# A hybrid decoder step on one core: single PSUM banks for two operands of a seven-product layer, and one table set for logarithm and exponential

## The chip, the cores and the metric

The kernel runs on one core of a Trainium2 chip. The core has five engines that work beside each other: TensorE (PE, the matmuls; PEld is its loading of weights), VectorE (DVE), ScalarE (ACT), GpSimd (POOL) and SyncE (SP, here an issuer of DMAs). Each engine takes its instructions in the order in which they stand in its own queue; semaphores make one engine wait for another. The metric is device microseconds (us) of one execution, as the median of several runs.

## The reference, cut to what matters

One inference step of a two-layer trunk, for a prompt of 512 tokens and 8 samples of one token, which share all weights. Here the two feed-forward halves of a trunk layer matter:

```
def rms_norm(x, g):
    y = x * lax.rsqrt(jnp.mean(x * x, axis=-1, keepdims=True) + EPS)
    return y * g

def swiglu(x, w_in, w_out):                  # w_in 1024 x 5632, w_out 2816 x 1024
    g, u = jnp.split(x @ w_in, 2, axis=-1)
    return (jax.nn.silu(g) * u) @ w_out

def trunk(x, ...):
    for l in range(2):
        x = x + 0.5 * swiglu(rms_norm(x, ffn1_g[l]), ffn1_w_in[l], ffn1_w_out[l])
        x = x + mixer_l(rms_norm(x, mix_g[l]))
        x = x + cross_attn(rms_norm(x, xattn_g[l]), ...)
        x = x + 0.5 * swiglu(rms_norm(x, ffn2_g[l]), ffn2_w_in[l], ffn2_w_out[l])
    return rms_norm(x, final_g)
```

The rest (a convolution and a gated recurrence as the mixer of the first layer, differential attention over paged caches as that of the second, cross-attention) is computed too, and the change does not touch its code, apart from the norm and the PSUM pool that all stages share.

## The kernel before, in words

**Tiles.** The 520 columns (512 prompt tokens, 8 samples) of x lie transposed in eight tiles of 128 x 520. Values are kept in two parts, a rounded high one and a low rest (`ah` and `al` of an activation, `whi` and `wlo` of a weight), so a product takes three passes: `ah,whi`, `al,whi` and `ah,wlo`. Each matmul handles 260 columns; a 520-column result takes a pair of PSUM banks. All eight banks are four such pairs, a pool (`psp`) from which every user takes a whole pair as one tile (`ps()`). What one instruction writes waits for those that still read *the tile*, whichever bank of it they read.

**Feed-forward layers.** Three of the four (`f1_0` and `f2_0` in trunk layer 0, `f1_1` in trunk layer 1) run through `ffn7` (L521). Each has 22 blocks of 128 hidden columns, in chunks of 8, 8 and 6 blocks. A chunk makes the hidden blocks first and then eight *output units*, one for each tile of x (`mm3` of 48 matmuls, `scaled` at L388, an addition to x). A hidden block is made in one of two ways:

- a *plain* one is a g unit and a u unit of 48 matmuls each (L353), then `scaled` of g (L388), Silu (L550), the product of both (L563) and its split into high and low parts (L373, L374). Plain are blocks 0, 1, 2, 8 and 16 of `f1_0` and `f2_0`, and 0, 8 and 16 of `f1_1`;
- a *seven-product layer* (`Seven.run`, 53 of them) makes g and u at once by Strassen's scheme in Winograd's form: seven products of 12 matmuls with sums of the weights (`sums`, `shi`, `slo`) and of the activations (`th`, `tl`) as operands, into four quarter results A, B, C and E. The first pair of banks is the tile `pa` (A and B, a bank each), the second `pc` (C and E).

In short, the order of the products, their destinations and what takes the results out:

```
self.product(A, w["a11"], b(0, 0), True)       # S.copy(g[:, lower], A)            L491
self.product(B, w["s1"], t(0), True)           # S.copy(u[:, upper], B)            L495
self.product(C, w["a12"], b(1, 0), True)       # V.tensor_add(g lower, .., C)      L498
self.product(A, w["s2"], t(1), False)          # S.copy(g[:, upper], A)            L501
self.product(B, w["s4"], b(1, 1), False)       # V.tensor_add, V.tensor_mul        L504, L505
self.product(E, w["a22"], t(3), True)          # S.activation Silu                 L508
self.product(A, w["s3"], t(2), False)          # S.copy, V.tensor_add, V.tensor_add L511 to L513
```

The matmuls of all products are at L472. Afterwards `rest()` multiplies g and u (L517) and splits the product. `Seven.prep` (L425) makes the operands of the next layer, in steps that `run` calls between the products: sums on DVE (L438, L441, L449, L453), casts to the high part on ACT (L439, L442, L446, L450, L455, L457, L461), low parts on DVE (L444, L452, L459, L462). `Seven.operands` (L405) makes the sums of the activations, in steps among the plain units of a first chunk.

**Norm.** `Norm.square` squares x on ACT (L320) and adds on DVE (L321); `_finish` sums over the partitions by two matmuls with a matrix of ones (L339), and makes the inverse root as exp(-0.5 ln(.)) on ACT (L341, L342), when `rstd()` is first asked for. ACT holds one table set of functions; where the next function is not in it, a table load (ACT_TABLE_LOAD) is put ahead.

**What sets the order.** A scheduler places the instructions of each engine by readiness and the order of the code. The products of the layers keep their order by `tc.issue_after`. `Weights` loads and splits weight tiles (L67, L78, L79) some steps ahead of their use, and a list of background work (parameters, at the start) is stepped by `bg.tick`.

Of the kernel before, what the change touches and what calls it, by code (L numbers as in the profile page):

```python
# [8 lines left out]
F32 = mybir.dt.float32  # L9
# [3 lines left out]
AF = mybir.ActivationFunctionType  # L13
# [3 lines left out]
P = 128  # L17
D = 1024
KT = 8
T = 512  # L20
# [30 lines left out]
def halves(ap, n):  # L51
    return ap.rearrange("p (s n) -> p s n", s=2, n=n)
# [122 lines left out]
def build(tc, a, outs):  # L175
# [11 lines left out]
    wspl = ctx.enter_context(tc.tile_pool(name="wspl", bufs=WB))  # L187
    psp = ctx.enter_context(tc.tile_pool(name="psp", bufs=4, space=bass.MemoryType.PSUM))
    drp = ctx.enter_context(tc.tile_pool(name="drp", bufs=1, space=bass.MemoryType.DRAM))
    tmp = ctx.enter_context(tc.tile_pool(name="tmp", bufs=TB))  # L190

    def ps():
        return psp.tile([P, 2, 512], F32, name="ps", tag="ps")

    def t2(name="t2"):
        return tmp.tile([P, TT], F32, name=name, tag="t2")
# [91 lines left out]
    class Norm:  # L288
# [25 lines left out]
        def square(self, k, c0=0, c1=TT):  # L314
            x = xT[k][:, c0:c1]
            if k == 0:
                S.activation(self.ss[:, c0:c1], x, AF.Square)
            else:
                sq = t2("sq")
                S.activation(sq[:, c0:c1], x, AF.Square)  # L320
                V.tensor_add(self.ss[:, c0:c1], self.ss[:, c0:c1], sq[:, c0:c1])  # L321
# [13 lines left out]
        def _finish(self, c0, c1):  # L335
            n = (c1 - c0) // 2
            p = ps()
            for s in range(2):
                PE.matmul(p[:, s, :n], ones, self.ss[:, c0 + s * n:c0 + (s + 1) * n], start=True, stop=True)  # L339
            sd = t2("sd")  # L340
            S.activation(halves(sd[:, c0:c1], n), p[:, :, :n], AF.Ln, bias=eps_t, scale=1.0 / D)  # L341
            S.activation(self._rstd[:, c0:c1], sd[:, c0:c1], AF.Exp, scale=-0.5)  # L342
# [42 lines left out]
    def scaled(p, rstd, name, out=None):  # L385
        n = rstd.shape[-1] // 2
        t = t2(name) if out is None else out
        V.tensor_mul(halves(t[:, :2 * n], n), p[:, :, :n], halves(rstd, n))  # L388
        return t

    class Seven:
# [85 lines left out]
        def run(self, nrm, w, step, before):  # L477
# [6 lines left out]

            pa, pc = ps(), ps()
            A, B, C, E = (p[:, s, :H2] for p in (pa, pc) for s in range(2))
            g, u = t2("g"), t2("u")
# [33 lines left out]
    def ffn7(tag, nrm, post, seven, chunks=CHUNKS, first=iter(())):  # L521

        plain = PLAIN[tag]
        for ci, (f0, nf) in enumerate(chunks):
# [14 lines left out]
            for f in range(f0, f0 + nf):  # L539
# [5 lines left out]
                if f in plain:  # L545
                    pg = ps()
                    for _ in mm3_gen(pg, ws.next((tag, "g", f)), nrm.act, H2):
                        step()
                    g = scaled(pg, nrm.rstd(), "g")
                    S.activation(g, g, AF.Silu)  # L550
                    wu = ws.next((tag, "u", f))
# [4 lines left out]
                    pu = ps()  # L556
                    for _ in mm3_gen(pu, wu, nrm.act, H2):
                        step()
# [106 lines left out]
    with ExitStack() as ctx1:  # L665
# [65 lines left out]
        nmix = Norm("mix", 0)  # L731
        seven = Seven(ctx1.enter_context(tc.tile_pool(name="seven", bufs=1)))
        ffn7("f1_0", n0, nmix.tile_, seven, first=(x for j in range(KT // 2) for x in seven.operands(n0, j)))
        bg.drain()

    def even_mixer(nrm, post):
# [674 lines left out]
    with tc.tile_pool(name="seven", bufs=1) as pool:  # L1411
        seven = Seven(pool)
        n1 = Norm("ffn1", 1, seven=seven)
        ffn7("f2_0", nf, n1.tile_, seven, first=(x for j in range(KT // 2) for x in seven.operands(nf, j)))
        nmix = Norm("mix", 1)
        ffn7("f1_1", n1, nmix.tile_, seven)

    def self_attn_sample(qs, ks, vs, pool, dst, ready, pages, page_order):
# [450 lines left out]
    with tc.tile_pool(name="fin", bufs=2) as pool:  # L1869
# [35 lines left out]
        V.tensor_scalar(ys, ys, r5[:NS, 4:5], None, op0=OP.mult)  # L1905
        S.dma_start(o_ys[:, 0, :], ys.rearrange("p s n -> p (s n)"))
    ctx.close()

# [33 lines left out]
```

## Time and profile before

| | us |
|---|---|
| median of 3 runs | 2598.58 |
| lowest and highest | 2596.54, 2598.66 |
| the profiled execution | 2599.44 |
| span of its trace | 2597.6 |

The profile is one execution, not the median. Its busy times are shares of the span: PE 93%, PEld 88%, DVE 66%, ACT 42%, POOL 10%. These are averages over stages that differ: among the seven-product layers DVE is far busier than in the output units. In the rows further down a matmul of 260 columns lasts 0.28 us, and the next one starts about 0.12 us after it did, so that matmuls overlap; the pace is read from starts. In brackets stands the idle time of an engine ahead of an instruction, and what ended it. The granted clock of PE is given as a share of its upper level: 1.00 is 2.4 GHz and 0.50 is 1.2 GHz.

### The profile page before, as it was taken

What the parts mean: (1) busy time and instruction counts of PE and PEld (TensorE: products, weight loads), DVE (VectorE), ACT (ScalarE), POOL (GpSimd) and SP (SyncE); (2) the same over time, 40 slices, a digit from 0 to 9 for tenths busy, and PEclk for the clock granted to TensorE, in tenths of its full rate; (3) what the DMA queues carried; (4) which work ended last, traced back from release to release, by engine and by line L of the source; (5) the groups of instructions that cost most, each with busy time, mean ns of one, the idle gap of its engine ahead of it and who ended that gap; (6) DMA issues with size and microseconds to landing.
All of it is one profiled execution on the core that took longest, in us unless ns stands there. A gap on an engine that the chain in (4) does not pass through costs nothing.

```text
span 2597.6 us, 49066 instructions
## 1 busy us (share of the span) xinstructions
PE 2425.3 (93%) x20642; PEld 2292.9 (88%) x20642; DVE 1706.8 (66%) x2800; ACT 1097.1 (42%) x1906; POOL 269.1 (10%) x340
## 2 busy tenths in 40 slices
PE   7998999999889998999898999999989899998998
PEld 7898989989868898989898989977889799997898
DVE  7767568995375858478858486699577663354334
ACT  6435244365435525246525244465543232321323
POOL 1000000001021000000000000122011423412410
PEclk9999999999999999999999999999999899998999
DMA  4232333264375323232323233577354766978972
GB/s 141 82 105 83 93 94 112 84 195 146 107 260 165 106 82 100 75 92 84 106 76 95 82 96 116 163 231 234 112 178 143 254 202 217 318 237 277 281 201 66
DMA packets 475150, 382.65 MB, mean 147 GB/s; under 512 B 13590, under 2 KB 435610, under 8 KB 474920
## 3 DMA queue, kind: packets, MB, share of 16 engines
q1 hardware_dynamic: 431456, 224.43, 30.2%
q0 software_dynamic: 43024, 153.93, 17.9%
q8 instruction: 162, 2.65, 0.4%
q10 hardware_dynamic: 448, 1.15, 0.1%
q14 instruction: 60, 0.49, 0.1%
HBM read 363.41 MB, written 16.55 MB: 146 GB/s over the span
## 4 chain that ended last, share of the span: by engine, by line
PE 49%; issue 11%; DVE 7%; DMA 6%; ACT 4%; POOL 1%; ACTq 0%; POOLq 0%; DVEq 0%; another core or an unknown queue 0%
PE ps L353 29%; PE ps L472 14%; DMA page<-in_cache_k_dram,idx 2%; DMA bq<-qxd 1%; DVE pr L1467 1%; PE ps L1525 1%; PE ps L1068 1%; DVE wlo L79 1%; PE ps L652 1%; POOL page L1136 1%; DVE sc L1458 1%; PE ps L1222 1%; ACT g L491 1%; DVE prx L1156 0%; PE ps L1255 0%
## 5 line engine op out<-in xcount | busy, mean ns | idle before, releaser
L353 PE MATMUL ps<-ah,whi 128*128 128x260 f32 (+1 forms) x3936 | 812.7, 288 | 25.0 <-ACT ah L311 9.3
L353 PE MATMUL ps<-al,whi 128*128 128x260 f32 (+1 forms) x3936 | 799.1, 284 | 7.3 <-DVE al L1775 2.6
L353 PE MATMUL ps<-ah,wlo 128*128 128x260 f32 (+1 forms) x3936 | 795.9, 284 | 3.3 <-DVE wlo L79 2.6
L353 PEld LDWEIGHTS ps<-ah,whi 128*128 128x128 f32 x3936 | 609.1, 190 | 49.0 <-issue 16.6
L353 PEld LDWEIGHTS ps<-al,whi 128*128 128x128 f32 x3936 | 610.8, 190 | 13.1 <-DVE al L312 3.1
L353 PEld LDWEIGHTS ps<-ah,wlo 128*128 128x128 f32 x3936 | 609.5, 190 | 7.0 <-DVE wlo L79 4.4
L78 ACT CAST whi<-wraw 128x1024 fp32r<-128x1024 f32 (+1 forms) x254 | 259.2, 1022 | 625.7 <-PE ps L353 443.0
L79 DVE TENSOR_TENSOR wlo<-wraw,whi 128x1024 fp32r<-128x1024 f32 (+1 forms) x254 | 301.4, 1188 | 94.7 <-ACT whi L78 93.1
L472 PE MATMUL ps<-th,shi 128*128 128x260 f32 x636 | 185.4, 292 | 29.4 <-ACT g L491 28.5
L472 PE MATMUL ps<-tl,shi 128*128 128x260 f32 x636 | 179.9, 283 | 0.0
L472 PE MATMUL ps<-th,slo 128*128 128x260 f32 x636 | 179.2, 282 | 0.0
L472 PEld LDWEIGHTS ps<-th,shi 128*128 128x128 f32 x636 | 119.3, 188 | 40.5 <-ACT g L491 39.2
L388 DVE TENSOR_TENSOR t<-ps,rstd 128x520 f32<-128x520 f32 x72 | 50.3, 698 | 131.3 <-PE ps L353 131.3
L652 PE MATMUL ps<-memT,wraw 128*128 128x256 f32 x512 | 122.5, 381 | 0.0
L472 PE MATMUL ps<-al,whi 128*128 128x260 f32 x424 | 120.0, 283 | 0.0
L472 PEld LDWEIGHTS ps<-th,slo 128*128 128x128 f32 x636 | 119.9, 189 | 0.0
L472 PE MATMUL ps<-ah,wlo 128*128 128x260 f32 x424 | 119.9, 283 | 0.0
L472 PEld LDWEIGHTS ps<-tl,shi 128*128 128x128 f32 x636 | 119.8, 188 | 0.0
L472 PE MATMUL ps<-ah,whi 128*128 128x260 f32 x424 | 119.8, 282 | 0.0
L652 PEld LDWEIGHTS ps<-memT,wraw 128*128 128x128 f32 x512 | 92.2, 190 | 10.2
L472 PE MATMUL ps<-ah,shi 128*128 128x260 f32 x212 | 65.7, 310 | 37.7 <-ACT g L501 37.7
L1427 POOL DMA_INDIRECT page<-in_cache_k_dram,idx x64 | 66.3, 1036 | 305.7 <-DVE pr L1467 179.8
(474 smaller groups left out, 4027.5 us busy)
## 6 DMA issues: line engine op xcount, KB each, us to landing
wraw<-in_ffn_w_in_dram SPq DMA_DIRECT2D x176, 512.0 KB
wraw<-in_ffn_w_out_dram SPq DMA_DIRECT2D x64, 512.0 KB
wraw<-in_xattn_w_kv_dram SPq DMA_DIRECT2D x32, 512.0 KB
page<-in_cache_mem_k_dram POOLq DMA_DIRECT2D x32, 512.0 KB
page<-in_cache_mem_v_dram POOLq DMA_DIRECT2D x32, 512.0 KB
page<-in_ffn_w_in_dram POOLq DMA_DIRECT2D x28, 512.0 KB
wraw<-in_ffn_w_out_dram SPq DMA_DIRECT2D x32, 384.0 KB
wraw<-in_attn_w_in_dram SPq DMA_DIRECT2D x24, 512.0 KB
```

Source lines behind the costliest of these rows:

```text
L78: self.nc.scalar.copy(hi[:, :nk], raw[:, :nk])
L79: self.nc.vector.tensor_sub(lo[:, :nk], raw[:, :nk], f32(hi[:, :nk]))
L353: PE.matmul(p[:, s, :n], w[:, j, :], x[:, s * n:(s + 1) * n], start=first and m == 0, stop=last and m == 2)
L388: V.tensor_mul(halves(t[:, :2 * n], n), p[:, :, :n], halves(rstd, n))
L472: e = PE.matmul(dst[:, :H2], wt[:, j, :], x, start=first and j == 0 and m == 0, stop=j == 3 and m == 2, skip_group_check=True)
L491: S.copy(g[:, lower], A)
L652: PE.matmul(p[:, 0, :256], w[:, k, :], memT[:, k, :], start=k == 0, stop=k == KT - 1)
L1068: PE.matmul(p[32 * j:32 * j + 32, o // 4, (o % 4) * P:(o % 4 + 1) * P], inp[:, k, :], w[:, k, :], start=(o % 4 == 0 and k < 4), stop=(k + ...
L1136: G.dma_start(tl, a[src][l, b, t * P:(t + 1) * P].rearrange("p h d -> p (h d)"))
L1222: PE.matmul(dst, self.q[dt][qi][:, qb * P:(qb + 1) * P], self.kp[:, ki, dt, :], start=n == 0, stop=n == 5, skip_group_check=True)
L1427: G.indirect_dma_start(out=t, out_offset=None, in_=src, in_offset=bass.IndirectOffsetOnAxis(ap=idx[:, b * 8 + j:b * 8 + j + 1], axis=0))
L1458: V.reduce_sum(sc[:, j, :].rearrange("p (m h b) -> p h m b", m=2, h=8)[:, :, :, b % 4], pr.rearrange("p (h m d) -> p h m d", h=8, m=2), ax ...
```

## The change

Four things are changed.

1. A function `banks(single)` closes the PSUM pool and opens it anew. With `single` there are two pairs (`psp`) and four single banks (`ps1`), otherwise four pairs as before. `banks(True)` stands ahead of `f1_0` and ahead of `f2_0`; `banks(False)` behind `f1_0` and behind `f1_1`.
2. In `Seven.run` A and B are single banks, a tile each; C and E remain a pair.
3. In `_finish`, where there are single banks, each of the two matmuls with ones has its own bank and its own logarithm of 260 columns. Behind the last square of a norm a preload names the table set `natural_log_exp_and_others`, which holds both functions.
4. In a plain block the scaling of g and its Silu are written into the loop over the u unit: behind the fifth of its eight steps in the first block of a chunk, behind the first step in the others. With the scaling goes `rstd()`, so in the first chunk `_finish` too.

```diff
@@ build
-    psp = ctx.enter_context(tc.tile_pool(name="psp", bufs=4, space=bass.MemoryType.PSUM))
+    psum = {"ctx": ExitStack()}
+
+    def banks(single):
+
+        psum["ctx"].close()
+        psum["ctx"] = ExitStack()
+        psum["two"] = psum["ctx"].enter_context(
+            tc.tile_pool(name="psp", bufs=2 if single else 4, space=bass.MemoryType.PSUM))
+        psum["one"] = None
+        if single:
+            psum["one"] = psum["ctx"].enter_context(tc.tile_pool(name="ps1", bufs=4, space=bass.MemoryType.PSUM))
+
+    banks(False)
...
     def ps():
-        return psp.tile([P, 2, 512], F32, name="ps", tag="ps")
+        return psum["two"].tile([P, 2, 512], F32, name="ps", tag="ps")
+
+    def ps1():
+        return psum["one"].tile([P, 512], F32, name="p1", tag="p1")
@@ Norm.square
-                S.activation(sq[:, c0:c1], x, AF.Square)
+                e = S.activation(sq[:, c0:c1], x, AF.Square)
+                if k == KT - 1 and self.hilo and c1 > T - 1 and c0 == 0:
+                    with tc.issue_after(e.ins):
+                        S.preload_act_table_set("natural_log_exp_and_others")
@@ Norm._finish
-            p = ps()
+            sd = t2("sd")
+            both = None if psum["one"] else ps()
             for s in range(2):
-                PE.matmul(p[:, s, :n], ones, self.ss[:, c0 + s * n:c0 + (s + 1) * n], start=True, stop=True)
-            sd = t2("sd")
-            S.activation(halves(sd[:, c0:c1], n), p[:, :, :n], AF.Ln, bias=eps_t, scale=1.0 / D)
+                c = slice(c0 + s * n, c0 + (s + 1) * n)
+                p = ps1() if both is None else both[:, s]
+                PE.matmul(p[:, :n], ones, self.ss[:, c], start=True, stop=True)
+                if both is None:
+                    S.activation(sd[:, c], p[:, :n], AF.Ln, bias=eps_t, scale=1.0 / D)
+            if both is not None:
+                S.activation(halves(sd[:, c0:c1], n), both[:, :, :n], AF.Ln, bias=eps_t, scale=1.0 / D)
@@ Seven.run
-            pa, pc = ps(), ps()
-            A, B, C, E = (p[:, s, :H2] for p in (pa, pc) for s in range(2))
+            A, B = ps1()[:, :H2], ps1()[:, :H2]
+            pc = ps()
+            C, E = (pc[:, s, :H2] for s in range(2))
@@ ffn7, a plain block
-                    g = scaled(pg, nrm.rstd(), "g")
-                    S.activation(g, g, AF.Silu)
                     wu = ws.next((tag, "u", f))
...
-                    for _ in mm3_gen(pu, wu, nrm.act, H2):
+                    for j, _ in enumerate(mm3_gen(pu, wu, nrm.act, H2)):
+                        if j == (4 if f == f0 else 0):
+                            g = scaled(pg, nrm.rstd(), "g")
+                            S.activation(g, g, AF.Silu)
                         step()
@@ the stages
+        banks(True)
         ffn7("f1_0", n0, nmix.tile_, seven, first=(x for j in range(KT // 2) for x in seven.operands(n0, j)))
         bg.drain()
+        banks(False)
...
+        banks(True)
         n1 = Norm("ffn1", 1, seven=seven)
         ffn7("f2_0", nf, n1.tile_, seven, first=(x for j in range(KT // 2) for x in seven.operands(nf, j)))
         nmix = Norm("mix", 1)
         ffn7("f1_1", n1, nmix.tile_, seven)
+        banks(False)
```

How the instructions stand now is shown at three places. The first is PE in the second seven-product layer of the first chunk of `f1_0`, where the first product ends and the second begins. Before, with `ps_843` the pair of A and B:

```order
L472 MATMUL ps_843<-ah_231,whi_731 128x260
L472 MATMUL ps_843<-al_232,whi_731 128x260
L472 MATMUL ps_843<-ah_231,wlo_732 128x260
L472 MATMUL ps_843<-th_313,shi_771 128x260
L472 MATMUL ps_843<-tl_314,shi_771 128x260
L472 MATMUL ps_843<-th_313,slo_772 128x260
```

Now, with `p1_854` the bank of A and `p1_855` that of B (the line of the matmuls is L495 there):

```order
L495 MATMUL p1_854<-ah_231,whi_742 128x260
L495 MATMUL p1_854<-al_232,whi_742 128x260
L495 MATMUL p1_854<-ah_231,wlo_743 128x260
L495 MATMUL p1_855<-th_321,shi_782 128x260
L495 MATMUL p1_855<-tl_322,shi_782 128x260
L495 MATMUL p1_855<-th_321,slo_783 128x260
```

The order is the same; the second product goes to another tile than the first.

The second place is ACT at the start of `f1_0`, behind the last square. Before:

```order
L320 ACTIVATE sq<-x_94 128x520
L78 CAST whi<-wraw 128x1024
L411 ACTIVATE tsc<-x_87,gains 128x2x260
L412 ACTIVATE xo<-x_88,gains 128x520
L412 ACTIVATE xo<-x_90,gains 128x520
L412 ACTIVATE xo<-x_92,gains 128x520
L412 ACTIVATE xo<-x_94,gains 128x520
L421 CAST th<-tsc 128x1040
L341 ACT_TABLE_LOAD
L341 ACTIVATE sd<-ps,eps_t 128x520
L342 ACT_TABLE_LOAD
L342 ACTIVATE rstd<-sd 128x520
```

Now (L335, L434, L435 and L444 are the lines L320, L411, L412 and L421 of before):

```order
L335 ACTIVATE sq<-x_94 128x520
L338 ACT_TABLE_LOAD
L78 CAST whi<-wraw 128x1024
L434 ACTIVATE tsc<-x_87,gains 128x2x260
L435 ACTIVATE xo<-x_88,gains 128x520
L435 ACTIVATE xo<-x_90,gains 128x520
L435 ACTIVATE xo<-x_92,gains 128x520
L435 ACTIVATE xo<-x_94,gains 128x520
L444 CAST th<-tsc 128x1040
L362 ACTIVATE sd<-p_426,eps_t 128x260
L362 ACTIVATE sd<-p_429,eps_t 128x260
L365 ACTIVATE rstd<-sd 128x520
```

One table load, directly behind the squares, stands for two, and the logarithm is in two halves. Over the whole program 41 table loads stand in ACT's listing, and 45 before. On PE the two matmuls with ones come 30 matmuls later than before, inside the first u unit; the same holds at the starts of `f2_0` and `f1_1`.

The third place is DVE among the first three plain blocks of `f1_0`, around the scaling of the second g. Before (L388 is that scaling, L563 the product of g and u of the first block):

```order
L438 TENSOR_TENSOR sums<-wraw 128x512
L388 TENSOR_TENSOR g<-ps,rstd 128x520
L415 TENSOR_TENSOR tsc<-tsc 128x260
L563 TENSOR_TENSOR u<-g,ps 128x520
L416 TENSOR_TENSOR tsc<-tsc,xo 128x520
L79 TENSOR_TENSOR wlo<-wraw,whi 128x1024
L417 TENSOR_TENSOR tsc<-xo,tsc 128x260
```

Now (L411 and L588 are L388 and L563 of before; L438 to L440 are L415 to L417, L461 is L438 and L464 is L441):

```order
L461 TENSOR_TENSOR sums<-wraw 128x512
L438 TENSOR_TENSOR tsc<-tsc 128x260
L411 TENSOR_TENSOR g<-ps,rstd 128x520
L439 TENSOR_TENSOR tsc<-tsc,xo 128x520
L79 TENSOR_TENSOR wlo<-wraw,whi 128x1024
L440 TENSOR_TENSOR tsc<-xo,tsc 128x260
L464 TENSOR_TENSOR sums<-wraw,sums 128x512
L588 TENSOR_TENSOR u<-g,ps 128x520
```

The scaling and the product are further apart, with the preparation of operands between them. The second u unit is written to the pair that this scaling reads; before, with four pairs, it went to another one. The queues of SP and POOL hold the same instructions in the same order as before.

## Rows read from the trace of the kernel before

**Rows 1.** Page, part 1: busy us, share of the span, instructions.

```profile
PE 2425.3 (93%) x20642; PEld 2292.9 (88%) x20642; DVE 1706.8 (66%) x2800; ACT 1097.1 (42%) x1906; POOL 269.1 (10%) x340
```

**Rows 2.** Who waited for L491 (first row) and L501 (second): us, times.

```profile
  PE ps L472: 28.5, 52
...
  PE ps L472: 37.7, 44
```

**Rows 3.** Windows: length; busy us (instructions) of PE, PEld, DVE, ACT, POOL; clock; DMA; GB/s.

```profile
1000.00:1025.00 25.00, 22.23 (x179) 21.40 (x179) 20.31 (x32) 13.80 (x29) 0.00 (x0) 1.00 0.32 88
1075.00:1100.00 25.00, 25.00 (x210) 25.00 (x210) 10.65 (x13) 4.94 (x5) 0.00 (x0) 1.00 0.34 101
25.00:50.00 25.00, 20.25 (x151) 19.86 (x152) 18.04 (x26) 20.23 (x27) 0.00 (x0) 0.86 0.15 43
```

**Rows 4.** Timeline, a seven-product layer: start, us, engine, line, out<-in [idle before <-releaser].

```profile
1001.25 0.28 PE L472 MATMUL ps<-ah,wlo 128*128 128x260 f32 x1
...
1002.05 0.39 PE L472 MATMUL ps<-th,shi 128*128 128x260 f32 x1 [0.52 <-ACT g L491]
...
1003.59 0.28 PE L472 MATMUL ps<-ah,whi 128*128 128x260 f32 x1
...
1003.85 0.38 ACT L495 COPY u<-ps 128x260 f32<-128x260 f32 x1 [1.85 <-PE ps L472]
...
1005.03 0.28 PE L472 MATMUL ps<-th,shi 128*128 128x260 f32 x1
...
1006.35 0.28 PE L472 MATMUL ps<-th,slo 128*128 128x260 f32 x1
...
1007.50 0.39 PE L472 MATMUL ps<-ah,shi 128*128 128x260 f32 x1 [0.86 <-ACT g L501]
...
1014.03 0.39 PE L472 MATMUL ps<-th,shi 128*128 128x260 f32 x1 [0.52 <-ACT g L491]
```

**Rows 5.** Timeline, first seven-product layer of `f1_0`: its first and second product.

```profile
61.59 0.28 PE L472 MATMUL ps<-ah,whi 128*128 128x260 f32 x1
...
65.33 0.39 PE L472 MATMUL ps<-th,shi 128*128 128x260 f32 x1 [1.53 <-ACT g L491]
```

**Rows 6.** Timeline, DVE in `f1_0`: the scaling of the second and third g.

```profile
46.94 0.69 DVE L388 TENSOR_TENSOR g<-ps,rstd 128x520 f32<-128x520 f32 x1
...
58.47 0.69 DVE L388 TENSOR_TENSOR g<-ps,rstd 128x520 f32<-128x520 f32 x1
```

**Rows 7.** Groups of DVE, 988 to 1046.65: busy, mean ns | idle before, releaser.

```profile
L459 DVE TENSOR_TENSOR slo<-sums,shi 128x1024 fp32r<-128x1024 f32 x5 | 6.1, 1225 | 2.5 <-ACT shi L457 2.5
...
L444 DVE TENSOR_TENSOR wlo<-wraw,whi 128x1024 fp32r<-128x1024 f32 x4 | 4.9, 1226 | 1.9 <-ACT whi L442 1.9
L374 DVE TENSOR_TENSOR al<-u,ah 128x520 fp32r<-128x520 f32 x5 | 3.5, 701 | 1.3 <-ACT ah L373 1.3
```

**Rows 8.** An L388 of an output unit; what L388 waited for (us, times).

```profile
1064.93 0.70 DVE L388 TENSOR_TENSOR t<-ps,rstd 128x520 f32<-128x520 f32 x1 [1.97 <-PE ps L353]
...
  PE ps L353: 278.0, 93
```

**Rows 9.** Timeline, the start of `f1_0`: the matmuls with ones and the inverse root.

```profile
29.75 2.10 PE L339 MATMUL ps<-ssum,ones 128*128 128x260 f32 x4 [5.54 <-DVE ssum L321]
...
32.47 1.28 ACT L341 ACT_TABLE_LOAD   x1
33.77 0.69 ACT L341 ACTIVATE sd<-ps,eps_t 128x520 f32<-128x520 f32 x1
34.48 1.28 ACT L342 ACT_TABLE_LOAD   x1
```

**Rows 10.** Timeline, the start of `f2_0`: its second u unit, its second and third L388.

```profile
838.18 0.51 PE L353 MATMUL ps<-ah,whi 128*128 128x260 f32 x2 [4.36 <-ACT whi L78]
...
841.05 0.69 DVE L388 TENSOR_TENSOR g<-ps,rstd 128x520 f32<-128x520 f32 x1
...
853.70 0.70 DVE L388 TENSOR_TENSOR g<-ps,rstd 128x520 f32<-128x520 f32 x1 [0.19 <-PE ps L353]
```

More of the change, by code (lines that the diff above doesn't have):

```diff
@@ L1906, in build @@
         S.dma_start(o_ys[:, 0, :], ys.rearrange("p s n -> p (s n)"))
+    psum["ctx"].close()
     ctx.close()
```

## The prediction

> **What bounds the kernel now.** I read the busy times first: TensorE (PE) is busy for 93% of the span, VectorE (DVE) 66%, ScalarE (ACT) 42% [rows 1]. Time comes off only where PE waits. Next I looked for the groups of PE with the largest idle time ahead of them: products whose first matmul is `th,shi` waited 52 times, 28.5 us in all, for the copy in L491, and products that start with `ah,shi` 44 times, 37.7 us, for the copy in L501 [rows 2]. These are the second and the fifth product of a seven-product layer; I call the products P1 to P7 in the order in which `Seven.run` issues them.
>
> Then the stretches. In 1000 to 1025 us, seven-product layers alone, PE gets 179 matmuls done; in 1075 to 1100 us, output units alone, 210, both at a granted clock of 1.00, the upper level of 2.4 GHz [rows 3]. What the layers lose is waiting, not clock. The timeline shows it [rows 4]: P1's last matmul starts at 1001.25 and another would follow 0.12 later (25 us by 210), at 1001.37; P2 starts at 1002.05, released by L491, the copy of P1's result. P2 writes the other bank of the pair, but both banks are one tile, so the write waits for that read. P4's last matmul starts at 1006.35; P5, due at 1006.47, starts at 1007.50, behind L501.
>
> **What a layer costs, and would cost.** P2 starts at 1002.05 and the next layer's at 1014.03: a period of 11.98 us [rows 4]. From P3 (1003.59) to P4 (1005.03) there is no wait: 1.44 us for a product, 10.08 for seven. The loss is 1.90 us a layer. P2's share is 0.68 ahead of it (1001.37 to 1002.05) and 0.10 in it (1002.05 to 1003.59 is 1.54, not 1.44): 0.78. I give the rest, 1.12, to P5.
>
> So 52 x 0.78 = 40.6 and 44 x 1.12 = 49.3 [rows 2]. P2's wait is 0.52 in the usual layer, and in the first layer of `f1_0` 1.53 [rows 4, 5], 1.0 more. **At most 90.9 us can be won here.** Of the 53 layers nine, the last of each chunk, show no wait at P5: there four matmuls of the first output unit stand ahead of it, and I count nothing for them.
>
> **Part by part.** (1) A and B become tiles of one bank each. P2 and P5 then write a tile that nobody reads. What is late next: P4 adds to A and needs L491, which has P2 and P3 (2.88 us) for a copy of 0.38 (L495's row [rows 4]); P5 needs L495, with P3 and P4 between; P7 needs L501, with P5 and P6 between. C and E stay a pair, so P6 still waits for DVE's addition out of C, again with two products between. Four single banks are two layers' worth, as now. I cost these waits at nothing. The cover is 2.88 us each; if ACT or DVE fell that far behind, the wait would come back under another name.
>
> (2) DVE must keep the new pace. It is busy for 20.31 of 25 us among the layers [rows 3]: 9.73 us in a period of 11.98. Against PE's 10.08 that fits, with 0.35 to spare: 97% full. In the five layers between 988 and 1046.65 us it waited for ACT casts 2.5 us ahead of L459, 1.9 ahead of L444 and 1.3 ahead of L374 [rows 7], 5.7 in all or 1.14 a layer. Those casts wait in ACT's queue among copies that wait for PE, and DVE prepares a layer ahead of its use; an in-order engine that runs a little behind finds its inputs ready. So I take it that DVE follows, and that it costs 1 us in each of the three first chunks, where it has the operands to prepare as well: 3 us. Both ends: 0, and the first rival below.
>
> (3) Pairs fall from four to two for plain and output units. In the output units DVE waits for PE ahead of L388 (1.97 at 1064.93) and reads a pair in 0.70 [rows 8]; the next use of that pair is a whole unit away. Nothing. But `f1_0` and `f2_0` begin with three plain units in a row, and there the second u unit takes the pair that its own g unit has just left, so PE would wait for L388 of that g. In the trace of before DVE comes to these at 46.94 and 58.47 in `f1_0` [rows 6]. P1 of the first layer starts at 61.59 [rows 5], and a unit of 48 matmuls takes 5.71; so the third u unit starts at 55.88 and the second at 44.46. With L388's 0.69 the waits would be 3.2 and 3.3. In `f2_0` the second u unit starts at 838.18, having waited 4.36 for its weights, and L388 starts at 841.05: 3.6; the third comes to 0.9, as DVE has waited for PE there (0.19 at 853.70 [rows 10]). Together 11 us if DVE comes no earlier, 3 or 4 if it comes as soon as the unit ends. In `f2_0` the first g unit also takes the pair of the last unit of the cross-attention output: about 1 us, an evacuation of 0.70 and its start.
>
> (4) Against that stands the start of `f1_0`. PE idles 5.54 us before the matmuls of the sum of squares (L339), then runs at half rate [rows 9]; the granted clock of 25 to 50 us is 0.86 [rows 3]. With L339 behind 30 matmuls of the first u unit (3.6 us) most of that hole is filled. The two table loads of logarithm and exponential (32.47 and 34.48, 1.28 each [rows 9]) become one, ahead of the sum. I count 3 us won in `f1_0` and 3 lost again at its two u waits, 4 lost in `f2_0` with the first g unit, and 1 for pauses of PE that lower the clock behind them, as the 5.54 us did. **Starts: 5 lost.** Bounds: 12 lost (all of (3)), 3 won.
>
> At 32.47 a table load took 1.28 us, and the ACTIVATE behind it began 1.30 us after its start [rows 9]. The Trainium skill (ScalarE: Activation LUTs, "What ACT_TABLE_LOAD costs") counts a drain of about 1.38 us on top of a load; by that price each start that loses a load would win 1.4 us more, and the sum would be 3 us lower. The row shows no such drain, and I go by the row.
>
> (5) Elsewhere four table loads fall away over the whole program (45 in the listing before, 41 after), 1.28 us each, on an ACT that is 42% busy. I take 0; bounds 3 either way.
>
> **Sum.** 90.9 - 3 - 5 = 82.9 us. From the profiled execution's 2599.44 us that gives 2516.5; it stands 0.86 above the median of the runs, so **2516 us**. Its own range is 2504 (all of 90.9, and 3 at the starts) to 2528 (12 lost at the starts and 1 us in each of nine chunks).
>
> **Rivals.** *DVE becomes the bound.* If its waits for casts (1.14) all stay, a layer takes 9.73 + 1.14 = 10.87 us instead of 10.08: 53 x 0.79 = 42 given back, 2558; with half of them 2537. For it: 97% load, and queues in order on two engines that wait for each other. Against it: the casts wait for PE themselves, and would come earlier. 24%, between 2529 and 2558.
>
> *The layers gain, and two pairs take more than that.* If L388 came so late that every plain and output unit waited for its evacuation as P2 did for L491 (0.78, and 0.32 more, since L388 takes 0.70 and the copy 0.38: 1.10), 72 output and 26 plain units would lose 108 us: 2599 - 91 + 108, and 8 of (2) and (4), 2624, slower. It decides from the point where DVE begins to read a pair more than 5 us, a unit less the evacuation, after its end. Against it: L388 waited for PE 93 times, 278 us in all [rows 8]; DVE is early there. 3%.
>
> *It doesn't do what it says.* P2 still waits, since PE may not write while ACT reads PSUM: no gain, about 2599. Against it: L495 copies out at 1003.85, while P3's matmuls go on [rows 4]. 2%. The Trainium skill (PSUM — Partial Sum Buffer, "PSUM bank collisions raise a hardware error") names a clash only within one bank and quadrant; by that rule the rival is out, and the row agrees.
>
> The forecast itself has 71%. **Range 2504 to 2546**: the forecast's own and the larger part of the DVE rival. A measurement of this kernel tells about 0.2% (5 us) from no change: faster by more than that 95%, within it 2%, slower 3%.
>
> **What would show it.** Right: no L491 and no L501 among PE's releasers in the layers; from P2 to P2 10.1 us, and 205 or more matmuls in 25 us there; DVE above 90% busy in the same stretch; waits of 1 to 4 us at the second and third u unit of `f1_0` and `f2_0`. Wrong: a period of 10.5 or more with PE behind `wlo` or `slo` (the DVE rival); waits for DVE's addition ahead of P6 (the cover in (1) was too thin); waits for L388 in the output units (the pairs).

## The result, and the profile after

The changed kernel takes 2505.22 us (median of 4 runs, 2499.38 to 2510.69), the kernel before 2597.56 beside it: a ratio of 0.9647, 95% interval 0.9622 to 0.9671, some 92 us. The prediction was 2516, with a range from 2504 to 2546. Run again later, the ratio was 0.9647 (0.9634 to 0.9661).

The profiled execution took 2510.69 us, the longest of the four; its span is 2508.9, 88.7 below the span before. The page's busy times, against [rows 1]:

```profile
PE 2396.1 (96%) x20642; PEld 2287.6 (91%) x20642; DVE 1696.5 (68%) x2800; ACT 1088.6 (43%) x1905; POOL 267.2 (11%) x340
```

The windows that answer to [rows 3]: a stretch of seven-product layers alone (the second chunk of `f2_0`, 36 us earlier than before), one of output units, and the start.

```profile
965.00:990.00 25.00, 25.00 (x211) 25.00 (x210) 24.43 (x38) 16.11 (x34) 0.00 (x0) 1.00 0.46 127
1025.00:1050.00 25.00, 25.00 (x210) 25.00 (x210) 10.84 (x14) 5.18 (x5) 0.00 (x0) 1.00 0.34 100
25.00:50.00 25.00, 22.36 (x179) 21.89 (x179) 19.65 (x29) 20.06 (x29) 0.00 (x0) 0.99 0.23 65
```

The layers get 211 matmuls done in 25 us, as many as the output units; before it was 179. PE is busy throughout, and DVE for 24.43 us of the 25. The timeline of one layer shows the same places as [rows 4] (`p` is a single bank, L495 the line of the matmuls, L515, L519 and L525 are L491, L495 and L501 of before):

```profile
965.52 0.28 PE L495 MATMUL p<-ah,wlo 128*128 128x260 f32 x1
965.65 0.28 PE L495 MATMUL p<-th,shi 128*128 128x260 f32 x1
...
966.09 0.37 ACT L515 COPY g<-p 128x260 f32<-128x260 f32 x1
...
969.60 0.28 PE L495 MATMUL p<-th,shi 128*128 128x260 f32 x1
...
969.96 0.28 PE L495 MATMUL p<-ah,shi 128*128 128x260 f32 x1
...
970.56 0.37 ACT L525 COPY g<-p 128x260 f32<-128x260 f32 x1
```

P2 starts 0.13 behind P1's last matmul, and the copy out of A runs while P2 goes on; P5 (969.96) is under way when the copy L525 begins. Nobody on PE waits for either copy any more.

What PE waits for instead, at the starts (L376 is L353, L411 is L388):

```profile
20.02 0.77 PE L376 MATMUL ps<-ah,whi 128*128 128x260 f32 x2 [6.14 <-ACT whi L78]
...
35.72 0.47 PE L376 MATMUL ps<-ah,whi 128*128 128x260 f32 x2 [0.57 <-DVE g L411]
...
43.77 0.48 PE L376 MATMUL ps<-ah,whi 128*128 128x260 f32 x2 [2.07 <-DVE g L411]
...
57.13 0.51 PE L376 MATMUL ps<-ah,whi 128*128 128x260 f32 x2 [0.64 <-DVE g L411]
...
389.32 0.48 PE L376 MATMUL ps<-ah,whi 128*128 128x260 f32 x2 [3.12 <-DVE t L411]
...
790.94 0.48 PE L376 MATMUL ps<-ah,whi 128*128 128x260 f32 x2 [1.33 <-ACT sq L335]
...
808.06 0.77 PE L376 MATMUL ps<-ah,whi 128*128 128x260 f32 x2 [4.52 <-DVE g L411]
```

**Where the time went.** The copy out of the first product (L491, now L515) marks each layer. From its starts in both traces:

| stretch | before | after | won |
|---|---|---|---|
| start of the program to the first copy | 64.91 | 64.39 | 0.5 |
| within the nine chunks, and over their output units to the next chunk of the same feed-forward layer (50 periods) | 940.1 | 850.1 | 90.0 |
| last copy of `f1_0` to the first of `f2_0` (mixer and cross-attention between) | 490.20 | 495.94 | -5.7 |
| last copy of `f2_0` to the first of `f1_1` | 63.33 | 59.04 | 4.3 |
| last copy of `f1_1` to the end | 1039.0 | 1039.4 | -0.4 |
| sum | 2597.6 | 2508.9 | 88.7 |

The last layer of a chunk with its output units won 1.07 on average, wherever it stands between two chunks of one feed-forward layer (68.66 against 67.60 in `f1_1`). The last three stretches hold such a layer each. Taken out, the layers won 90.0 + 3.2 = 93.2; the way from `f1_0` to `f2_0` lost 6.8, the start of `f1_1` won 3.2 and the tail lost 1.5. Another execution of the changed kernel (`e0`) has 850.0 within the chunks, 497.5 from `f1_0` to `f2_0` and 1034.6 in the tail: the 90.0 is firm, the way to `f2_0` is known to some 2 us, and the tail says nothing.

### The profile page after: what moved, and what is told of

Its sections match the earlier page's. It is cut to its first block, busy times and chain, and to the rows that moved or that the text cites. A ratio compares the mean times of both kernels' runs of the same rounds, so it can differ in the third digit from the quotient of the medians.

```text
span 2508.9 us, 49098 instructions
## 1 busy us (share of the span) xinstructions
PE 2396.1 (96%) x20642; PEld 2287.6 (91%) x20642; DVE 1696.5 (68%) x2800; ACT 1088.6 (43%) x1905; POOL 267.2 (11%) x340
## 4 chain that ended last, share of the span: by engine, by line
PE 65%; DVE 13%; issue 9%; DMA 8%; ACT 4%; POOL 2%; ACTq 0%; POOLq 0%; another core or an unknown queue 0%; DVEq 0%
PE ps L376 38%; PE p L495 15%; PE ps L495 6%; DVE bigah L827 2%; DVE wlo L79 2%; DMA page<-in_cache_k_dram,idx 2%; DVE pr L1496 1%; DMA bq<-qxd 1%; PE ps L1554 1%; DMA wraw<-in_ffn_w_in_dram 1%; PE ps L1095 1%; PE ps L677 1%; POOL page L1163 1%; DVE sc L1487 1%; PE ps L1249 1%
## 5 line engine op out<-in xcount | busy, mean ns | idle before, releaser
L376 PE MATMUL ps<-ah,whi 128*128 128x260 f32 (+1 forms) x3936 | 815.9, 289 | 38.7 <-ACT whi L78 8.1
L376 PE MATMUL ps<-al,whi 128*128 128x260 f32 (+1 forms) x3936 | 799.9, 284 | 7.7 <-DVE al L1289 4.4
L376 PE MATMUL ps<-ah,wlo 128*128 128x260 f32 (+1 forms) x3936 | 796.7, 284 | 1.5 <-DVE wlo L79 1.0
L376 PEld LDWEIGHTS ps<-ah,whi 128*128 128x128 f32 x3936 | 611.1, 191 | 64.0 <-issue 24.2
L376 PEld LDWEIGHTS ps<-al,whi 128*128 128x128 f32 x3936 | 612.9, 190 | 12.1 <-DVE al L1289 5.1
L376 PEld LDWEIGHTS ps<-ah,wlo 128*128 128x128 f32 x3936 | 611.2, 190 | 4.1 <-issue 2.3
L78 ACT CAST whi<-wraw 128x1024 fp32r<-128x1024 f32 (+1 forms) x254 | 259.2, 1021 | 634.3 <-PE ps L376 451.9
L79 DVE TENSOR_TENSOR wlo<-wraw,whi 128x1024 fp32r<-128x1024 f32 (+1 forms) x254 | 301.2, 1187 | 96.8 <-ACT whi L78 94.3
L495 PE MATMUL p<-tl,shi 128*128 128x260 f32 x636 | 179.6, 282 | 0.0
L495 PE MATMUL p<-th,shi 128*128 128x260 f32 x636 | 179.5, 282 | 0.0
L495 PE MATMUL p<-th,slo 128*128 128x260 f32 x636 | 179.4, 282 | 0.0
L411 DVE TENSOR_TENSOR t<-ps,rstd 128x520 f32<-128x520 f32 x72 | 50.2, 697 | 134.6 <-PE ps L376 134.6
L495 PEld LDWEIGHTS p<-th,slo 128*128 128x128 f32 x636 | 119.9, 188 | 0.0
L495 PEld LDWEIGHTS p<-tl,shi 128*128 128x128 f32 x636 | 119.5, 188 | 0.0
L495 PEld LDWEIGHTS p<-th,shi 128*128 128x128 f32 x636 | 119.4, 188 | 0.0
L1456 POOL DMA_INDIRECT page<-in_cache_k_dram,idx x64 | 65.6, 1024 | 304.4 <-DVE pr L1496 177.6
L1496 DVE TENSOR_TENSOR pr<-page,bq 128x1024 f32<-128x1024 f32 x64 | 78.1, 1221 | 26.7 <-DMA page<-in_cache_k_dram,idx 20.1
L396 ACT CAST ah<-u 128x520 fp32r<-128x520 f32 (+1 forms) x88 | 55.1, 627 | 76.8 <-DVE u L541 29.9
L827 DVE SCALAR_TENSOR_TENSOR bigah<-ue,cw,bigah 128x512 f32<-128x512 f32 x120 | 82.8, 739 | 0.2
L1456 POOL DMA_INDIRECT page<-in_cache_v_dram,idx x64 | 66.1, 1033 | 132.0 <-PE ps L1554 83.3
```

The source lines that it names most:

```text
L78: self.nc.scalar.copy(hi[:, :nk], raw[:, :nk])
L79: self.nc.vector.tensor_sub(lo[:, :nk], raw[:, :nk], f32(hi[:, :nk]))
L376: PE.matmul(p[:, s, :n], w[:, j, :], x[:, s * n:(s + 1) * n], start=first and m == 0, stop=last and m == 2)
L396: S.copy(hi[:, c0:c1], src[:, c0:c1])
L495: e = PE.matmul(dst[:, :H2], wt[:, j, :], x, start=first and j == 0 and m == 0, stop=j == 3 and m == 2, skip_group_check=True)
L827: V.scalar_tensor_tensor(acc[i][:, :T], ue[:, i, t:t + T], cw[:, t, i:i + 1], acc[i][:, :T], op0=OP.mult, op1=OP.add)
```

## The experiments

**Which part carries the gain.** `e1` keeps the PSUM tiles of the change and takes back the preload and the moved scaling:

```diff
-                e = S.activation(sq[:, c0:c1], x, AF.Square)
-                if k == KT - 1 and self.hilo and c1 > T - 1 and c0 == 0:
-                    with tc.issue_after(e.ins):
-                        S.preload_act_table_set("natural_log_exp_and_others")
+                S.activation(sq[:, c0:c1], x, AF.Square)
...
+                    g = scaled(pg, nrm.rstd(), "g")
+                    S.activation(g, g, AF.Silu)
                     wu = ws.next((tag, "u", f))
...
-                    for j, _ in enumerate(mm3_gen(pu, wu, nrm.act, H2)):
-                        if j == (4 if f == f0 else 0):
-                            g = scaled(pg, nrm.rstd(), "g")
-                            S.activation(g, g, AF.Silu)
+                    for _ in mm3_gen(pu, wu, nrm.act, H2):
                         step()
```

> The changed kernel without the preload of the table set and with the scaling of g (and the sum of squares with it) back ahead of the u unit: only the PSUM tiles are changed. Theory (one tile for A and B made P2 and P5 wait): nearly the whole gain stays. The hole ahead of the matmuls with ones in f1_0 comes back (5.5 us, and its half rate) and the start of f1_1 loses what it gained (3 us): about 2511 us, 2507 to 2516, no ACT copy among PE's releasers in the layers. Rival (preload and moved scaling carry a large part of the 92 us): above 2530.

Measured: 2511.07 us against 2601.35 before, ratio 0.9657 (0.9640 to 0.9673). The tiles alone carry the gain; of the copies only that out of B stands among PE's releasers in the layers, once, with 0.3 us. The time is as expected, and so is the start of `f1_1` (63.07 us from `f2_0`, 59.04 with all of the change). The hole in `f1_0` did not come back: PE waits 0.31 us ahead of the matmuls with ones (L357 there),

```profile
29.04 0.49 PE L357 MATMUL p<-ssum,ones 128*128 128x260 f32 x1 [0.31 <-DVE ssum L336]
```

and the first copy out of A starts at 66.19, only 1.8 behind the changed kernel's 64.39. PE pauses for 5.52 us further ahead, before the first unit (19.98), where the pool is opened.

`e2` is the other half, the kernel before with the preload and the moved scaling, four pairs and a shared A and B:

> The kernel before with the preload and the moved scaling alone; A and B share a pair, four pairs throughout. Theory: the layers stay at 12.0 us with the waits behind L491 and L501; only the starts of f1_0 and f1_1 gain, 4 to 10 us in all: about 2591. Rival (as for e1): below 2570.

Measured: 2582.27 against 2601.35, ratio 0.993 (0.9914 to 0.9947), 19 us, about twice what was expected. The layers keep their 12.0 us. In `f1_0` the first copy starts at 54.94 instead of 64.91: 10 us. The timeline of `e2` shows the matmuls with ones (L342 there), the counterpart of the first line of [rows 9]:

```profile
28.66 1.11 PE L342 MATMUL ps<-ssum,ones 128*128 128x260 f32 x4 [0.45 <-DVE ssum L324]
```

Of 5.54 us of idling 0.45 are left, and the granted clock of 25 to 50 us is 1.00 (the upper level) against 0.86 in [rows 3]:

```profile
25.00:50.00 25.00, 24.55 (x202) 24.26 (x202) 22.88 (x33) 22.84 (x33) 0.00 (x0) 1.00 0.30 85
```

202 matmuls instead of 151. From `f1_0` to `f2_0` 3.6 us are won (490.20 to 486.59), to `f1_1` 3.3 (63.33 to 60.08).

`e2b` has the moved scaling without the preload, `e6` the changed kernel without the preload.

> The kernel before with the moved scaling alone, four pairs, no preload. Preload and move together had given 19 us there, with the first copy out of f1_0 at 54.9 instead of 64.9 us. Theory (the move fills the hole of 5.5 us ahead of the matmuls with ones and the half rate behind it): 12 to 17 of the 19, the first copy at 55 to 59, about 2584. Rival (the preload carries at least half): 2588 or more.

Measured: 2591.14 against 2599.36, ratio 0.9974 (0.9963 to 0.9985): 8 us, not 12 to 17. The rival holds: the preload carries half. In `f1_0` the move alone wins most (first copy at 57.59, 7.3 of the 10 us). On the way to `f2_0` the move by itself is 2.1 slower (492.33), where both together win 3.6. PE waits there for weights (1.45 for a cast L78 at 831.80, 1.22 for a low part L79 at 840.33) and not for the scaling; why is open, and two executions of the changed kernel differ by 1.6 on this way.

> The changed kernel without the preload of the table set alone. Theory (the preload takes two loads of 1.28 us out of the way of the scaling of the first g, and nothing else of it is on the path): 2 to 4 us more at the starts of f1_0 and of f2_0 each, 4 to 8 in all, about 2511. Rival (its loads stand in the way elsewhere): 1 to 3 us less.

Measured: 2514.33, against 2507.74 for the changed kernel on the same chip (`e0`); ratios to the kernel before 0.967 and 0.9647. 6.6 us, as expected; the traces have 1.4, 2.6 and 1.9 of it at the starts of `f1_0`, `f2_0` and `f1_1`. At `f2_0` PE waits 6.03 for the scaling of the first g instead of 4.92 in `e0`, and 2.86 more for the second.

**Tile or bank.** `e5` changes one line of the kernel before:

```diff
-            A, B, C, E = (p[:, s, :H2] for p in (pa, pc) for s in range(2))
+            A, E, B, C = (p[:, s, :H2] for p in (pa, pc) for s in range(2))
```

> The kernel before with four pairs, but A shares its pair with E and B with C. Nothing else differs. Theory (a write waits for the reads of its tile): P2 no longer waits for the copy out of A, P5 no longer for the copy L501; but P3 writes C right behind P2 and waits for the copy out of B (L495), 0.78 a layer. So 44 x 1.12 = 49 us are won and P2's 41 are only moved: about 2548 us, 2543 to 2556, period about 10.9. Rival (the waits come from ACT reading PSUM at all, whatever the tile): no change, about 2597.

Measured: 2551.63 against 2601.35, ratio 0.981 (0.9793 to 0.9828). The period is 10.85 us, and PE's waits in the layers have moved to P3:

```profile
PE ps L472 <- ACT u L495: 35.8, 44, 2.9
```

Columns: us in all, times, longest. A shares its pair with E now, and P2 and P5 go into B while A is copied out: both start without a wait. P3 writes C, and waits for the copy out of B that shares C's pair. So a write waits for the reads of its tile, and PE writes one bank while ACT reads another. The split of the 1.90 us into 0.78 and 1.12 is right: 11.98 - 1.12 is 10.86.

**VectorE's room.** `e3` repeats the last low part of the weights once or twice a layer (the result is the same):

```diff
             V.tensor_sub(l22, a22, f32(h22))
+            V.tensor_sub(l22, a22, f32(h22))
```

> The changed kernel with one more VectorE subtraction of 512 elements a layer (the last low part of the weights, L462 of the kernel before, made twice; 0.60 us from start to start). In the changed kernel the 15 VectorE instructions of a layer take 9.6 to 9.7 us from starts against a period of 9.93 to 10.09. Theory (VectorE keeps pace with 0.3 to 0.45 us to spare, PE is the bound): 10.2 to 10.3 a layer, 0.15 to 0.3 more, 53 layers, less what a chunk's start has in hand: 2 to 14 us more, about 2513. Rival (VectorE is the bound already): 53 x 0.6 = 32 more, 2537. Rival (it has room of a us or more): no change.

> The same with two such subtractions a layer, 1.2 us. Theory: 10.8 to 10.9 a layer, 0.75 to 0.85 more, 53 layers, less what the chunks have in hand: 25 to 42 us more, about 2540; PE then waits for wlo or slo. Rival (already the bound): 64 more, 2569. Rival (room of a us or more): under 12 more.

Measured: 2508.43 and 2513.28 against 2598.26, ratios 0.9648 (0.9625 to 0.967) and 0.9664 (0.9643 to 0.9686). The first ratio is that of the changed kernel (0.9647), and its time can't tell the theory from no change. The traces can: within the chunks and their output units (850.1 in the table) `e3` takes 854.1 and 858.8 us, 3.9 and 8.7 more. The first lies in the range of the theory; the second lies far below it, where the rival with a us of room had it. So 1.2 us more work in each of 53 layers cost 9 us and not 25 to 42. A window of `e3_dve_two` in the second chunk of `f1_1`, and one in the output units ahead of it:

```profile
1310.00:1360.00 50.00, 50.00 (x417) 49.84 (x416) 50.00 (x80) 30.97 (x64) 0.00 (x0) 1.00 0.33 96
1255.00:1290.00 35.00, 35.00 (x293) 35.00 (x293) 15.58 (x19) 6.71 (x7) 0.00 (x0) 1.00 0.31 91
```

DVE is busy all the time and gets 80 instructions done in 50 us; at 17 a layer that is 4.7 layers, while PE with 417 matmuls does 5.0. DVE falls behind by some 0.3 layers in that stretch and PE does not wait. In the output units DVE has 15.58 us of work in 35 and catches up. The backlog reaches PE in seven layers, where P6 waits for the addition out of C: one at the start of the second and of the third chunk of `f1_0` (0.97 and 1.47) and of the third of `f2_0` (0.28), and four in the first chunk of `f1_1` (0.90 to 1.26, periods of 11.3 to 11.6).

**Pairs and openings of the pool.** `e4` trades two of the four single banks for a third pair:

```diff
-            tc.tile_pool(name="psp", bufs=2 if single else 4, space=bass.MemoryType.PSUM))
+            tc.tile_pool(name="psp", bufs=3 if single else 4, space=bass.MemoryType.PSUM))
...
-            psum["one"] = psum["ctx"].enter_context(tc.tile_pool(name="ps1", bufs=4, space=bass.MemoryType.PSUM))
+            psum["one"] = psum["ctx"].enter_context(tc.tile_pool(name="ps1", bufs=2, space=bass.MemoryType.PSUM))
...
-            A, B = ps1()[:, :H2], ps1()[:, :H2]
+            self.flip = not self.flip
+            if self.flip:
+                A, B = ps1()[:, :H2], ps1()[:, :H2]
+            else:
+                B, A = ps1()[:, :H2], ps1()[:, :H2]
```

> The changed kernel with three pairs and two single banks instead of two and four; from layer to layer A and B change places between the two banks, so that P1 writes the bank that B left two products earlier, and P2 that of A. Theory (two pairs cost some 10 us at the u units of f1_0 and f2_0 and at the last output units of f1_0, and the copy and addition out of A behind P7 are done 1.4 us later, when P2 starts): those waits go, about 2495 us, 2491 to 2503. Rival: DVE runs behind in the layers and the addition out of A comes late, so that P2 waits 0.2 to 0.4 us in each: 2505 to 2517, no better than the changed kernel.

Measured: 2508.55 against 2601.35, ratio 0.9644 (0.9628 to 0.9661): no better than the changed kernel, as the rival had it. The start of `f1_0` gains 4.6 us (first copy at 59.80) and the way to `f2_0` 3.2 (492.78), and the layers give it back. Around P2 of one layer:

```profile
973.83 0.28 PE L496 MATMUL p<-ah,wlo 128*128 128x260 f32 x1
974.09 0.39 PE L496 MATMUL p<-th,shi 128*128 128x260 f32 x1
974.32 0.28 PE L496 MATMUL p<-tl,shi 128*128 128x260 f32 x1
```

P2 starts 0.26 behind P1's last matmul and its second matmul 0.23 behind that, where 0.12 would do: 0.25 a layer, behind the addition out of A (periods of 10.3 from P2 to P2 there, instead of 10.05 to 10.09).

`e10` opens the single banks ahead of the pairs, so that the first pair has other banks:

> The changed kernel, only the place of the pools in PSUM differs: the single banks are opened first (banks 0 to 3), the two pairs behind them (4 to 7). Theory (a reopened pool gives its first pair the banks that were used last: the first g unit of f1_0 waits for the last transposes, 6.1 us with half the clock behind it, and the first unit behind f1_0 for the last output unit, 3.1): both waits go, 7 to 11 us less, about 2496. The u units of f1_0 and f2_0 still wait for the scaling of g. Rival (those waits have another cause, weights or the operands): no change, 2503 to 2507.

Measured: 2507.70 against 2598.26, ratio 0.9657 (0.9635 to 0.9679). No gain, and the waits stay:

```profile
20.38 0.77 PE L376 MATMUL ps<-ah,whi 128*128 128x260 f32 x2 [5.52 <-DVE x L725]
...
389.59 0.77 PE L376 MATMUL ps<-ah,whi 128*128 128x260 f32 x2 [3.09 <-DVE t L411]
```

My theory of the place falls: which banks the first pair has does not matter. The time is the rival's, though neither weights nor operands are the cause. The releasers are still the last copies out of the pool that was closed (the input's transposes, the last output unit). `e9` and `e11` tell whether it is the opening: the pool is opened only ahead of the first seven-product layer and closed ahead of the last output units (the other calls of `banks` at the stages go in the same way, and the order of the pools is that of `e10`).

```diff
                 else:
+                    if psum["one"] is None:
+                        rest()
+                        banks(True)
                     todo = seven.prep(tag, f + 1, nxt) if f + 1 < f0 + nf else outs()
...
+            if ci == len(chunks) - 1:
+                banks(False)
             r = nrm.rstd()
...
-        banks(True)
         ffn7("f1_0", n0, nmix.tile_, seven, first=(x for j in range(KT // 2) for x in seven.operands(n0, j)))
```

> As before this one, single banks first, and four pairs stay during the first plain blocks of f1_0, f2_0 and f1_1 and come back for the last output units of each of the three; the single banks are opened only for the seven-product layers between. Theory (the layers' gain of 93 us and the 19 us of preload and moved scaling add up, once two pairs no longer delay the starts): 2597 - 93 - 19 + 3 for the openings, about 2488, 2483 to 2495. Rival (opening the pool in the middle costs as much as two pairs do): 2497 to 2506.

Measured: 2505.17 against 2598.26, ratio 0.964 (0.962 to 0.966), hardly less than the changed kernel and in the range of the rival. But the trace shows both halves of it: without an opening there the first unit of `f1_0` starts at 15.58, not 20.02, and by the first copy of `f2_0` 14.9 us are won against the changed kernel (822.96, 837.85). The opening ahead of `f1_1` takes 8 back (67.10 from the last copy of `f2_0`, 59.04 in the changed kernel):

```profile
1164.38 0.56 PE L495 MATMUL p<-ah,whi 128*128 128x260 f32 x1 [6.38 <-DVE u L588]
```

`e11` leaves that one out (`if ci == len(chunks) - 1 and tag != "f2_0"`).

> The kernel of the run before this (single banks opened ahead of the first seven-product layer, four pairs during the first plain blocks) without the closing and opening between f2_0 and f1_1, which are one stretch again as in the changed kernel. Theory (each opening makes its first user wait for what the old pool still has in use; the one at the start of f1_1 cost 8 us): the first layer of f1_1 comes 59 us after the last of f2_0 instead of 67, and what was won at the starts of f1_0 and f2_0 (14 us by the last layer of f2_0) stays to the end: 12 to 15 us below the changed kernel, about 2492. Rival (what is won there is given back elsewhere behind the layers): within 5 us of the changed kernel.

> The changed kernel itself, as it is, beside the other runs of this batch on the same chip. Both theories: a ratio of 0.962 to 0.967 to the kernel before, some 2505 us.

Measured on one chip: `e11` 2494.00 (2491.29 to 2497.66, 5 runs), the changed kernel (`e0`) 2507.74 (2503.54 to 2511.68, 5 runs), the kernel before 2599.36; ratios 0.9597 (0.9583 to 0.961) and 0.9647 (0.9634 to 0.9661). `e11` beats both kernels, the changed one by 13.7 us. Its first layer of `f1_1` comes 59.13 us behind the last of `f2_0`. The ratios of the two halves, `e1` and `e2`, make 0.9657 x 0.993 = 0.959 together: `e11` gets what both promise (PE still waits 1.66 and 4.56 us in it ahead of the first layers of `f1_0` and `f2_0`), and the changed kernel gave some 14 us of it away at its openings and to its two pairs. With a third pair and the same openings `e4` has 7.8 of it back at the starts.

## Why the prediction was right, and where it was not

The forecast's mechanism is the one that the runs show. The time lies in the range, 1.2 us above its lower end, and one of the four executions (2499.38) lies below it. Against the 82.9 us of the forecast the traces have 88.7: the layers won 5.3 more (the 3 us for DVE, which did not show, and 2.3 at the ends of the chunks), the starts lost 1.9 less, and the tail lost 1.5. The medians have 92, as the profiled execution was the longest. By its own steps:

**What a layer costs.** Right. P2's 0.78 and P5's 1.12 are what `e5` separates. (A and B are results of the products, not operands, as the title has it.) At most 90.9 us were to be won; the layers won 93.2. The 44 periods within the chunks won 83.6, which is 44 x 1.90. The surplus stands in the last layers of the nine chunks, for whose P5 I counted nothing. Before, P5 of such a layer starts 0.27 behind the matmul ahead of it, and its second matmul 0.23 behind that, where 0.12 would do:

```profile
1054.65 0.40 PE L353 MATMUL ps<-al,whi 128*128 128x260 f32 x2
1055.04 0.39 PE L472 MATMUL ps<-ah,shi 128*128 128x260 f32 x1
1055.27 0.28 PE L472 MATMUL ps<-al,shi 128*128 128x260 f32 x1
```

That is 0.26 a layer (the second of the two L353 starts at 1054.77), and nine of them are 2.3 us.

From P2 to P2 a layer without a wait now takes 10.05 to 10.09 us behind the first of each chunk, as forecast. Where the copies out of A stand closer, as in the second chunk of `f1_0` (9.94), it is ACT that catches up:

```profile
192.91 0.28 PE L495 MATMUL p<-th,shi 128*128 128x260 f32 x1
193.92 0.37 ACT L515 COPY g<-p 128x260 f32<-128x260 f32 x1
...
202.96 0.28 PE L495 MATMUL p<-th,shi 128*128 128x260 f32 x1
203.86 0.38 ACT L515 COPY g<-p 128x260 f32<-128x260 f32 x1
```

P2 starts 10.05 apart; the copy comes 1.01 behind the first and 0.90 behind the second. The period of 9.93 that stands in the expectation of `e3` is one of copies.

**The cover of the other waits** (1). Right: P4, P6 and P7 do not wait for the copies and additions; P5 waited twice for the copy out of B, 0.8 us in all.

**DVE** (2). The 97% came out as 98% (24.43 of 25), and that DVE follows was right. The 3 us for the first chunks did not show: that of `f2_0` won 8.9 where five P2 and four P5 come to 8.4, that of `f1_0` 8.0. The rival's price was the wrong step. I multiplied an excess per layer by 53, as if DVE had to be level with PE in every layer. It need not: it prepares a layer ahead, loses some of that lead in a chunk (0.3 layers in 50 us of `e3_dve_two`), and catches up in the output units. `e3_dve_two` charged it 1.2 us a layer and paid 9 us in all; by that, 0.79 a layer would hardly have come near the 42 us of the rival. The 24% were too many.

**The starts** (3) and (4). The sum, 5 us lost, is close (0.5 won, 6.8 lost, 3.2 won: 3.1 lost, known to some 2 us), but by luck: its terms were off, and cancel.
- The hole ahead of the matmuls with ones was put at 3 us; with four pairs preload and move are worth 10 in `f1_0` alone (`e2`), as the half rate behind the hole goes with it. In the changed kernel the hole is not there to be filled: with neither of them PE waits 0.31 at that place (`e1`), and both are worth 1.8. The 3.3 us at the start of `f1_1` (`e2`) were not in the sum at all.
- The opening of the pool was overlooked. The first unit of `f1_0` starts at 20.02; before, it started at 15.72. The first unit behind `f1_0` waits 3.12. `e10` and `e9` put that on the opening, not on the banks. The row at 20.02 names a cast of weights, which ends at 19.93; the last copy out of the closed pool ends at 19.88, and before the unit ran without either.
- In `f1_0` the u units waited 2.07 and 0.64, not 3.2 and 3.3: DVE came to the scaling of the second g at 42.92, 4 us earlier than in [rows 6].
- In `f2_0` I had the wait at the second u unit, behind the scaling of its g. It is one unit earlier: the second g unit takes the pair of the first g, whose scaling waits for the inverse root (808.06, 4.52 us). I did not ask who needs that pair next. The moved scaling is not the reason: `e1`, without the move, has the wait too (L373 and L408 are L376 and L411).

```profile
809.79 0.56 PE L373 MATMUL ps<-ah,whi 128*128 128x260 f32 x1 [4.28 <-DVE g L408]
```

Behind the pause ahead of 808.06 (first row) and the one ahead of 20.02 (second), both in the changed kernel, PE runs at the lower level of its clock, 1.2 GHz:

```profile
808.00:813.00 5.00, 4.94 (x23) 4.97 (x24) 3.39 (x4) 3.89 (x5) 0.00 (x0) 0.50 0.17 47
20.00:25.00 5.00, 4.98 (x23) 5.00 (x24) 4.79 (x7) 5.00 (x10) 0.00 (x0) 0.50 0.40 113
```

23 matmuls in 5 us instead of 42 (210 in 25 us): 19 x 0.12 or some 2.3 us more for each of the two pauses. The 1 us that I had for the clock was one pause at less than half its price.

**Table loads** (5). Weighed at 0; the preload is worth 6.6 us (`e6`), at the starts, where the loads stood ahead of the scaling that PE waits for. The price of one load is right: the load by the preload lasts 1.28 us in the changed kernel too (26.12). The Trainium skill (ScalarE: Activation LUTs, "What ACT_TABLE_LOAD costs") adds a drain; in `e6` a load at 34.25 starts 0.02 behind the end of the logarithm and the exponential starts at 35.55, 1.30 behind the load, so the trace shows none.

**The other rivals.** In the 72 output units L411 waits for PE as L388 did (134.6 us in all, 131.3 before), so DVE is early there and two pairs cost next to nothing; the 3.12 us behind the last unit of `f1_0` belong to the opening. That the wait would stay, since PE may not write while ACT reads, is out by [rows 4]'s counterpart and by `e5`.

## What to carry to other kernels

Look for two results that share a tile where one is read out while the next is written: the wait followed the tile here, not the bank, and re-pairing the results (`e5`) shows in one line what each wait is worth. When a buffer pool is shrunk or reopened, list at every start who takes which buffer next and what must have left it, moved reads included, and count the slow clock behind each pause; keep reopenings away from places where the engine that sets the time has no other work. An engine at 97% beside a full one was no bound here, as it works ahead and has a stretch to catch up: price its excess less the lead that a stretch starts with.

## What the runs showed of the hardware

Behind PE's pauses of 4.52 and 6.14 us in the changed kernel the granted clock was 0.50, the lower level, for 5 us (808 to 813 and 20 to 25 us), which adds some 2.3 us to each. Behind the first layer of a chunk, the 84 matmuls of a layer that waits for nothing took 10.05 to 10.09 us at a granted clock of 1.00. A VectorE instruction's record is longer than its share: 1024 elements are recorded with 1.22 us and, where it waits for nothing, the next one starts 1.14 behind (changed kernel, median of 274).
